# A decoder step on one core: the first block's conditioning made in two halves, with half granules of the input projection behind each

## The chip, the core and the metric

One core of a Trainium2 chip runs the whole step as one program. The metric is the device time of one execution in microseconds (us), from the first to the last instruction and what lies around them. All data is fp32. A product of two fp32 matrices is made of three matmuls on rounded parts (hi x wh, lo x wh, hi x wl), each with 128 x 128 weights and 288 moving columns.

## The reference, cut to what matters

```python
sc = jax.nn.silu(c)                                   # c: 9 sequences x 2048
mod = jnp.einsum('bd,sde->sbe', sc, w_ada[l]) + b_ada[l][:, None, :]
sh0, scl0, gt0 = jnp.split(mod[0], 3, axis=-1)        # shift, scale, gate, 2048 each
h = modulate(rmsnorm(x, norm_pre[l, 0]), sh0, scl0)   # h = xn * (1 + scale) + shift
proj = h @ w_in                                       # 288 rows, 2048 -> 6160
```

There are 256 prompt rows and 32 sample rows. This document is about the first microseconds: the modulation of layer 0's first sub-layer (w_ada), the modulated activations h, and their product with w_in. Everything later (attention, state-space layer, two MLPs) is unchanged.

## The kernel before

Activations lie with features on partitions: x is eight tiles ("pairs") of 128 x 2 x 288, so 256 features each. Four blocks of 512 features (two pairs) are numbered kb = 0 to 3. Weights come from memory in granules of 512 x 512 (1 MB, a tile raw of 128 x 4 x 512, 8 KB in a row per partition). split_w casts half a granule on ScalarE (wh) and subtracts on VectorE or, for the second half, on GpSimd (wl). gran_mm makes half a granule's output columns (pr = 0 or 1, a PSUM pair of two banks): 24 matmuls for a whole granule's four feature chunks; a granule is 48.

**Conditioning.** The shift and the scale of one block of 512 features are two times four granules of w_ada, 8 MB. ada_mm makes a step of one granule: four fp32 matmuls that lie side by side in four 32-column strips of the array and sum in one PSUM bank over the eight steps. ada_end then copies the bank to SBUF (ScalarE), turns it by four transposes (TensorE), reduces (VectorE) and ada_out makes the tiles mod A and mod B. For block 0 this is the generator first = ada_group(...), driven from the loop "for n in range(8)" that also loads x and sums its squares (Stat); r is the reciprocal norm. It loads through rawp, three buffers of a whole granule. For all later blocks it is the stream cond = ada_stream(groups, ...), whose tiles alternate between rawp and one buffer raw2; each next(cond) makes one step and sets off the load two steps ahead. ended tells which groups are complete.

**Projections.** The list slots sets the order: first eight granules (u = 0 to 7) of block 0, then eight of block 1, each closed alone (start = stop = 1): block 0 copies the PSUM pair to an SBUF accumulator proj (A.copy), block 1 adds to it (V.tensor_add). Later slots sum longer in PSUM. In front of slot 0, make_block(0) builds h of the two pairs, its rounded parts hi and lo (split_a); low_rank(kb) is a small product at the first slot of each block. The orders of TensorE and of SyncE, which issues all loads, are written out by hand (manual_schedule); those of ScalarE, VectorE and GpSimd are a planner's. fill_in puts 0.42 steps of cond at each of four points of a slot (i < 15). At the end of slots 6, 14 and 15 the stream is driven until the next block's group has ended, and make_block builds that block. The load of slot i+2 is issued and slot i+1 is split at the start of slot i. SyncE stands still at a load whose buffer is not free, with all later loads behind it.

Of the kernel before, what the change touches and what calls it, by code (L numbers as in the profile page):

```python
# [9 lines left out]
F32 = mybir.dt.float32  # L10
# [3 lines left out]
OP = mybir.AluOpType  # L14
AX = mybir.AxisListType
# [5 lines left out]
NT = NP + NB * TS  # L21
# [8 lines left out]
V_ADA = 0  # L30
V_PRE = 192
V_POST = 256
# [129 lines left out]
def build(tc, nc, d):  # L162
    mm = nc.tensor.matmul
# [67 lines left out]
    def split_a(t):  # L231
        hi = c2("hi", F32R)
        A.copy(hi, t)  # L233
        lo = c2("lo", F32R)
        V.tensor_sub(lo, t, hi.bitcast(F32))  # L235
        return hi, lo
# [15 lines left out]
    def chunks(pairs):  # L252
        return [(hi[:, c, :], lo[:, c, :]) for hi, lo in pairs for c in range(2)]
# [10 lines left out]
    def ada_src(blocks, n):  # L264
        l, s, nb = blocks[n // 4]
        return d["g_ada"][l, s, nb, n % 4]
# [12 lines left out]
            ada_out(blk, red[:, :, 9 * slot:9 * slot + 9])  # L279
        yield  # L280

    def ada_out(blk, v):
        l, s, nb = blk
        k0 = V_ADA + (l * 2 + s) * 48 + 4 * nb
        b = vec[:, k0:k0 + 4][:, :, None].to_broadcast([128, 4, 9])
        eb = nb % 4
        g0 = (l * 2 + s) * 16 + 4 * eb
        sl = slice(4 * eb, 4 * eb + 4)
        if nb < 4:
            V.tensor_add(mod("B", l, s)[:, sl, :], v, b)  # L290
            return
        t = ep.tile([128, 4, 9], F32, name=nm("adat"), tag="adat", bufs=2)
        V.tensor_add(t, v, b)
        if nb < 8:
            w = vec[:, V_PRE + g0:V_PRE + g0 + 4][:, :, None].to_broadcast([128, 4, 9])
            V.scalar_tensor_tensor(mod("A", l, s)[:, sl, :], t, 1.0, w, op0=OP.add, op1=OP.mult)
        else:
            w = vec[:, V_POST + g0:V_POST + g0 + 4][:, :, None].to_broadcast([128, 4, 9])
            V.tensor_mul(mod("G", l, s)[:, sl, :], t, w)

    def ada_group(blocks):
        ps = bank()
        for n in range(4 * len(blocks)):
            raw = load(ada_src(blocks, n))
            ada_mm(ps, blocks, n, raw)
            if n < 4 * len(blocks) - 1:
                yield
        for _ in ada_end(ps, blocks):
            pass
        yield 0  # L310
# [46 lines left out]
    ended = set()  # L357

    def drain(gen, n=10 ** 9):
        for _ in range(n):  # L360
            if next(gen, "end") == "end":
                break
# [83 lines left out]
    def make_h(p, r, l, s, act=False):  # L446
        t = h_norm(p, r)
        h_mod(t, p, l, s, act)
        return t
# [252 lines left out]
    x = []  # L702
# [5 lines left out]
        return t  # L708

    st = Stat(7)  # L710
    first = ada_group([(0, 0, 0), (0, 0, 4)])
    for n in range(8):
        if n < 4:
            x += [x_load(d["xT"], p) for p in (2 * n, 2 * n + 1)]
        if 2 <= n < 6:
            for p in (2 * n - 4, 2 * n - 3):
                st.add(x[p])
        if n == 6:
            r = st.rstd(keep=True)
        drain(first, 1)  # L720
    drain(first)


    def kgran_(hv, acts, acc, u, first, done=None):
# [456 lines left out]
    def w_load(i):  # L1181
        if i < len(slots):
            k, u, kb = slots[i][:3]
            raws[i] = load(d[k][u, kb])

    def w_split(i):
        if i < len(slots):
            hvs[i] = split_w(raws.pop(i), 2, (None, G))

    hops = {}  # L1190
    hts = {}

    def make_block(kb):
        hops[kb] = []
        for pp in range(2):
            t = make_h(2 * kb + pp, r, 0, 0, act=True)
            x[2 * kb + pp] = None
            hops[kb].append(split_a(t))
            hts[2 * kb + pp] = t

    def low_rank(kb):
        gp = bank((128, NT))
# [24 lines left out]
    def step(g, n=1):  # L1227
        for _ in range(n):
            next(g, None)
# [20 lines left out]
    att = attention()  # L1250
    m = Mlp(0)
    with tc.manual_schedule(engines={mybir.EngineType.PE, mybir.EngineType.SP}):
        w_load(0)
        w_load(1)
        step(cond, 3)
        make_block(0)
        w_split(0)
        for i, (k, u, kb, start, stop, init, fin) in enumerate(slots):
            inp = k == "g_in"
            w_load(i + 2)  # L1260
            if i == OUT + 6:
                sub.weights()
            m.before(len(slots) - 1 - i)
            if 0 <= i - OUT - 8 < 4:
                x[2 * (i - OUT - 8):2 * (i - OUT - 8) + 2] = [x_load(d["xT"], 2 * (i - OUT - 8) + k) for k in range(2)]
            if i == 14:
                sm = cst(C_SMASK)
                causal = cst(C_CAUSAL, 384)
            if inp and u == 0:
                low_rank(kb)  # L1270
            w_split(i + 1)
            if i + 1 in (OUT, OUT + 8):
                for nkb in ((0, 1) if i + 1 == OUT else (2, 3)):
                    while 2 * nkb + 1 not in mixed or nkb // 2 not in ready:
                        step(att)
                    oacts[nkb] = chunks([split_a(mixed.pop(2 * nkb + n)) for n in range(2)])
            hv = hvs.pop(i)
            acts = chunks(hops[kb]) if inp else oacts[kb]
            acc = proj if inp else yacc
            for pr in range(2):  # L1280
                pi = 2 * u + pr
                if start:
                    ps[pr] = pair()
                gran_mm(ps[pr], hv, pr, acts, start, stop, 0)
                fill_in(i)
                gran_mm(ps[pr], hv, pr, acts, start, stop, 1)
                if stop:
                    o_ = ps[pr][:, :, :NT]
                    if init:
                        acc[pi] = c2("acc")  # L1290
                        A.copy(acc[pi], o_)
                    else:
                        V.tensor_add(acc[pi], acc[pi], o_)  # L1293
                    if fin and inp:
                        projected(pi, acc[pi])
                    elif fin:
                        late.append(pi)
                fill_in(i)
            if i in (6, 14, 15):
                n = {6: 1, 14: 2, 15: 3}[i]  # L1300
                while n - 1 not in ended:
                    next(cond)
                make_block(n)
            while len(late) > 2:
                pi = late.pop(0)
                sub.add(pi, yacc[pi])
        while late:
            pi = late.pop(0)
            sub.add(pi, yacc[pi])
        drain(cond)  # L1310
# [639 lines left out]
```

## Time and profile before

| | |
|---|---|
| median of 3 runs | 2856.94 us (2851.47 to 2861.42) |
| the profiled execution, its own time | 2850.12 us |
| its span, first to last instruction | 2848.4 us |
| granted TensorE clock, mean | 0.978 |
| TensorE busy | 2725.4 us, 96% of the span |
| moved by DMA | 662.99 MB |

Times in the rows are microseconds from the start of the span. PE is TensorE, DVE VectorE, ACT ScalarE, POOL GpSimd, SP SyncE; an operation is named by its line, its output tile and its input tiles. A clock of 1.0 is full speed, 0.5 half speed. A DMA share of 1.0 says that all 16 DMA engines are busy.

### The profile page before, as it was taken

The numbers are of one execution on the slowest core, as the hardware profiler recorded it, in microseconds if no ns is written. First come the engines' busy times: TensorE is split into PE (matmuls) and PEld (weight loads), VectorE is DVE, ScalarE is ACT, GpSimd is POOL, SyncE is SP. The second block draws the span as 40 slices with busy tenths as digits, with TensorE's granted clock in tenths as the row PEclk, the third lists the DMA queues.
The fourth block names the chain that finished last, engine by engine and source line by source line (L and its number), as shares of the span: only waits on it lengthen the run. The fifth ranks groups of instructions, "written<-read, shape, count | busy, mean of one in ns | idle before, by whom it ended". The sixth has DMA issues, their size and how long they took to land.

```text
span 2848.4 us, 53282 instructions
## 1 busy us (share of the span) xinstructions
PE 2725.4 (96%) x22334; PEld 2458.7 (86%) x22334; DVE 1740.8 (61%) x2656; ACT 1079.6 (38%) x1389; POOL 381.8 (13%) x478
## 2 busy tenths in 40 slices
PE   6999998999999999999999799997999999999997
PEld 3788786777999999999999578874899999999997
DVE  2356556547866657687775767757545555555556
ACT  3344433334433333333433343333433333333332
POOL 1233242340010000000011322102000000000003
PEclk8999999999999999999999799998999999999998
DMA  9887686675677767765555698866564444444442
GB/s 351 341 320 296 261 283 240 240 291 196 251 253 245 260 237 281 274 240 196 189 192 198 223 323 304 311 240 250 197 236 165 168 169 165 163 163 165 169 170 93
DMA packets 167233, 662.99 MB, mean 233 GB/s; under 512 B 21440, under 2 KB 41280, under 8 KB 108368
## 3 DMA queue, kind: packets, MB, share of 16 engines
q1 hardware_dynamic: 158000, 633.56, 61.8%
q0 software_dynamic: 7840, 23.67, 2.1%
q8 instruction: 175, 2.87, 0.4%
q10 hardware_dynamic: 1152, 2.36, 0.2%
q14 instruction: 66, 0.54, 0.1%
HBM read 622.74 MB, written 36.77 MB: 232 GB/s over the span
## 4 chain that ended last, share of the span: by engine, by line
PE 85%; DVE 6%; DMA 5%; issue 2%; ACT 1%; POOL 1%; SPq 0%; POOLq 0%; DVEq 0%; ACTq 0%
PE mm L248 25%; PE mm L250 24%; PE mm L249 24%; PE b L260 5%; DMA raw<-g_ada 1%; PE b L1683 1%; DMA adaw<-g_ada 1%; DVE wl L227 1%; DMA raw<-g_glu 1%; PE b L1753 1%; PE b L1471 1%; DMA x<-xT 1%; PE b L1758 0%; PE b L494 0%; ACT wh L225 0%
## 5 line engine op out<-in xcount | busy, mean ns | idle before, releaser
L248 PE MATMUL mm<-hi,wh 128*128 128x288 f32 x5632 | 1693.7, 301 | 26.2 <-DVE acc L735 11.9
L249 PE MATMUL mm<-lo,wh 128*128 128x288 f32 x5632 | 1669.2, 296 | 4.5 <-DVE lo L611 4.4
L250 PE MATMUL mm<-hi,wl 128*128 128x288 f32 x5632 | 1668.1, 296 | 2.3 <-DVE wl L227 1.8
L248 PEld LDWEIGHTS mm<-hi,wh 128*128 128x128 f32 x5632 | 1062.9, 189 | 166.0 <-issue 98.6
L225 ACT CAST wh<-raw 128x1024 fp32r<-128x1024 f32 x692 | 719.3, 1049 | 1066.5 <-PE mm L249 859.6
L227 DVE TENSOR_TENSOR wl<-raw,wh 128x1024 fp32r<-128x1024 f32 x628 | 765.5, 1231 | 548.4 <-ACT wh L225 539.4
L249 PEld LDWEIGHTS mm<-lo,wh 128*128 128x128 f32 x5632 | 1064.6, 189 | 6.3 <-DVE lo L611 5.7
L250 PEld LDWEIGHTS mm<-hi,wl 128*128 128x128 f32 x5632 | 1063.5, 189 | 3.7 <-DVE wl L227 3.0
L735 DVE TENSOR_TENSOR acc<-acc,mm 128x576 f32<-128x576 f32 x304 | 227.8, 751 | 148.4 <-PE mm L250 147.5
L227 POOL TENSOR_TENSOR wl<-raw,wh 128x1024 fp32r<-128x1024 f32 x64 | 163.7, 2559 | 364.0 <-ACT wh L225 343.8
L260 PE MATMUL b<-raw,cpad 128*32 128x512 f32 x1104 | 156.1, 639 | 27.9 <-DMA raw<-g_ada 27.7
L482 POOL TENSOR_TENSOR acc<-acc,modG 128x512 f32<-128x512 f32 x32 | 39.4, 1231 | 979.1 <-ACT sq L391 836.9
L660 DVE TENSOR_TENSOR relu<-relu 128x576 f32<-128x576 f32 x64 | 48.3, 755 | 67.4 <-ACT relu L659 67.4
L260 PEld LDWEIGHTS b<-raw,cpad 128*32 128x32 f32 x1104 | 22.3, 110 | 60.0 <-issue 30.2
L1293 DVE TENSOR_TENSOR acc<-acc,mm 128x576 f32<-128x576 f32 x40 | 30.0, 751 | 70.0 <-PE mm L250 70.0
L659 ACT ACTIVATE relu<-mm 128x576 f32<-128x576 f32 x64 | 41.5, 649 | 79.7 <-PE mm L250 79.5
L233 ACT CAST hi<-relu 128x576 fp32r<-128x576 f32 x64 | 43.2, 675 | 72.4 <-DVE relu L660 72.4
L260 PE MATMUL b<-adaw,cpad 128*32 128x512 f32 x432 | 66.2, 651 | 0.8 <-DMA adaw<-g_ada 0.8
L235 DVE TENSOR_TENSOR lo<-relu,hi 128x576 fp32r<-128x576 f32 x64 | 48.3, 755 | 29.4 <-ACT hi L233 28.7
L1499 POOL DMA_DIRECT2D s5k<-lag x16 | 12.1, 756 | 284.8 <-ACT lag L1498 158.9
L1560 POOL DMA_DIRECT2D s5c<-lc x32 | 17.4, 543 | 225.8 <-DVE lc L1559 219.9
L1683 PEld LDWEIGHTS b<-h,rb 128*128 128x128 f32 x256 | 35.9, 220 | 12.4 <-ACT h L1673 7.9
(356 smaller groups left out, 1588.1 us busy)
## 6 DMA issues: line engine op xcount, KB each, us to landing
raw<-g_ada SPq DMA_DIRECT2D x138, 1024.0 KB, 5.2
raw<-g_up SPq DMA_DIRECT2D x128, 1024.0 KB, 4.8
raw<-g_dn SPq DMA_DIRECT2D x128, 1024.0 KB, 4.9
adaw<-g_ada SPq DMA_DIRECT2D x216, 256.0 KB, 6.3
raw<-g_in SPq DMA_DIRECT2D x48, 1024.0 KB, 6.8
raw<-g_glu SPq DMA_DIRECT2D x64, 512.0 KB, 6.6
raw<-g_out SPq DMA_DIRECT2D x16, 1024.0 KB, 6.7
s5b<-ft SPq DMA_DIRECT2D x128, 64.0 KB, 4.1
```

Source lines behind the costliest of these rows:

```text
L225: A.copy(wh, r)
L227: (lo[hf] or V).tensor_sub(wl, r, wh.bitcast(F32))
L233: A.copy(hi, t)
L235: V.tensor_sub(lo, t, hi.bitcast(F32))
L248: mm(o, wh[:, k4 % n, cs], hi, start=first and k4 == 0, stop=False)
L249: mm(o, wh[:, k4 % n, cs], lo, start=False, stop=False)
L250: mm(o, wl[:, k4 % n, cs], hi, start=False, stop=last and k4 == nk - 1)
L260: mm(ps[32 * k4:32 * k4 + 32, :], cpad[:, 4 * kg + k4, 18 - 9 * slot:50 - 9 * slot], raw[k4] if isinstance(raw, list) else raw[:, k4, :], ...
L659: A.activation(t, ps[pr][:, :, :NT], AF.Relu)
L660: V.tensor_mul(t, t, t)
L735: V.tensor_add(acc[pi], acc[pi], ps[:, :, :NT])
L1683: mm(vps[ch][ri][:, q, :], rb[q // 2][:, q % 2, ri, :], h4[p][:, q, c, :], start=True, stop=True)
```

## The change

first and second are now generators of ada_half: the same eight steps, each for 256 of the 512 output features. A step's tile comes as two loads of 128 x 2 x 256 (256 KB each, 1 KB in a row) into general SBUF tiles, up to three steps ahead, not into rawp. The sum over the steps takes 256 columns of a PSUM bank; two transposes follow, and ada_out writes half a block's mod A and B. After the first half, only pair 0 is built; eight half granules (the 256 features of pair 0, 12 matmuls for each pr, loads of 512 KB) run with one half step of second behind each (two behind the first), then pair 1 is built, low_rank(0) follows, and eight half granules of pair 1 add to proj. In these the steps of cond run, three for every two half granules, and cond starts only there. Slots 0 to 7 of the list fall away; slot 8 goes on as before.

```diff
+    def ada_half(blocks, hf, depth=3):
+        ps = bank()
+        held = []
+        def ahead(n):
+            if n < 4 * len(blocks):
+                ts = [c2("adaw", shape=(128, 2, 256)) for _ in range(2)]
+                for k, t in enumerate(ts):
+                    nc.sync.dma_start(t, ada_src(blocks, n)[:, 2 * k:2 * k + 2, 256 * hf:256 * hf + 256])
+                held.append(ts)
+        for n in range(depth):
+            ahead(n)
+        yield
+        for n in range(4 * len(blocks)):
+            ts = held.pop(0)
+            slot, kg = divmod(n, 4)
+            for k4 in range(4):
+                mm(ps[32 * k4:32 * k4 + 32, :256], cpad[:, 4 * kg + k4, 18 - 9 * slot:50 - 9 * slot], ts[k4 // 2][:, k4 % 2],
+                   start=n == 0, stop=n == 4 * len(blocks) - 1, tile_position=(0, 32 * k4))
+            ahead(n + depth)
+            yield
+        ev = c2("adae", shape=(128, 256))
+        A.copy(ev, ps[:, :256])
+        yield
...
-    first = ada_group([(0, 0, 0), (0, 0, 4)])
-    for n in range(8):
+    first, second = (ada_half([(0, 0, 0), (0, 0, 4)], hf) for hf in range(2))
+    for n in range(10):
...
-        w_load(0)
-        w_load(1)
-        step(cond, 3)
-        make_block(0)
-        w_split(0)
...
+        half_load(0)
+        half_load(1)
+        drain(second, 1)
+        drain(first)
+        hops[0] = []
+        make_pair(0, 0)
+        half_split(0)
+        for j in range(16):
+            part, u = divmod(j, 8)
+            half_load(j + 2)
+            if j == 7:
+                drain(second)
+                make_pair(0, 1)
+                drain(cond, 1)
+            if j == 8:
+                low_rank(0)
+            half_split(j + 1)
+            hv = hhv.pop(j)
+            for pr in range(2):
+                pi = 2 * u + pr
+                o_ = pair()
+                gran_mm(o_, hv, pr, chunks([hops[0][part]]), True, True)
+                o_ = o_[:, :, :NT]
+                if part:
+                    V.tensor_add(proj[pi], proj[pi], o_)
+                else:
+                    proj[pi] = c2("acc")
+                    A.copy(proj[pi], o_)
+                if pr and not part:
+                    drain(second, 2 if j == 0 else 1)
+                elif part and (pr or j % 2):
+                    step(cond)
+            if j == 14:
+                while 0 not in ended:
+                    next(cond)
+                make_block(1)
         for i, (k, u, kb, start, stop, init, fin) in enumerate(slots):
+            if i < 8:
+                continue
...
-            if i in (6, 14, 15):
-                n = {6: 1, 14: 2, 15: 3}[i]
+            if i in (14, 15):
+                n = {14: 2, 15: 3}[i]
```

half_load(j) loads half granule j into the first half of a rawp buffer (from j = 16 on: w_load(j - 8), a whole granule); half_split(j) splits it, with the subtraction on GpSimd for odd j. The slots 8 and on are reached with the stream's budget at zero.

## Rows read from the trace of the kernel before

**Rows 1.** Table by stage: start:end, length, busy times (instructions), clock, DMA share, GB/s.

```profile
0.00:28.00 28.00, 12.06 (x56) 2.96 (x56) 6.86 (x12) 11.35 (x18) 0.97 (x5) 1.00 0.92 356
28.00:45.50 17.50, 9.10 (x44) 1.99 (x44) 8.41 (x15) 6.79 (x9) 3.75 (x2) 0.52 0.95 377
45.50:80.00 34.50, 33.78 (x249) 26.48 (x246) 5.89 (x5) 10.17 (x13) 8.55 (x4) 1.00 0.90 334
80.00:114.80 34.80, 34.80 (x257) 27.63 (x255) 14.50 (x18) 15.54 (x21) 10.01 (x4) 1.00 0.90 339
```

**Rows 2.** Chain of work that ended last, first 50 us: start, duration, what.

```profile
24.66 7.42 DMA raw<-g_ada
32.13 1.98 PE b L260 x8
34.13 0.59 ACT adae L270
34.77 1.13 PE b L274 x4
35.92 0.70 DVE adar L277
...
37.21 0.60 ACT h L440
...
38.65 0.68 ACT hi L233
...
39.35 2.62 DVE lo L235
```

**Rows 3.** TensorE's timeline: start, duration, operation, times, idle time before it.

```profile
40.80 1.94 PE L260 MATMUL b<-raw,cpad 128*32 128x512 f32 x8 [4.92 <-DMA raw<-g_ada]
...
44.93 0.66 PE L1207 MATMUL b<-h,wglr 128*32 128x288 f32 x8
45.52 0.40 PE L248 MATMUL mm<-hi,wh 128*128 128x288 f32 x1
...
57.93 0.30 PE L249 MATMUL mm<-lo,wh 128*128 128x288 f32 x1
58.06 0.29 PE L250 MATMUL mm<-hi,wl 128*128 128x288 f32 x1
...
62.45 0.29 PE L250 MATMUL mm<-hi,wl 128*128 128x288 f32 x1
62.67 1.06 PE L260 MATMUL b<-raw,cpad 128*32 128x512 f32 x8
...
63.91 0.30 PE L249 MATMUL mm<-lo,wh 128*128 128x288 f32 x1
...
114.82 0.69 PE L1207 MATMUL b<-h,wglr 128*32 128x288 f32 x8
```

**Rows 4.** VectorE's timeline, the first modulated pair: start, duration, operation.

```profile
25.66 0.76 DVE L432 TENSOR_TENSOR h<-x,r 128x576 f32<-128x576 f32 x1
```

**Rows 5.** DMA view of 11 to 20 us, where all 16 engines are busy.

```profile
DMA packets 941, 3.80 MB, mean 422 GB/s; under 512 B 109, under 2 KB 109, under 8 KB 621
```

**Rows 6.** DMA view of 1546.5 to 1551.5 us: loads with rows of 2 KB.

```profile
DMA packets 1115, 2.02 MB, mean 405 GB/s; under 512 B 127, under 2 KB 127, under 8 KB 1115
```

**Rows 7.** The tile raw from 36 to 115 us: count, duration ns min/median/max, first and last start.

```profile
L260 PE MATMUL b<-raw,cpad x128: 592/617/1063, 40.8 to 112.5; 128*32 128x512 f32 x128
...
L225 ACT CAST wh<-raw x17: 1028/1048/1059, 37.7 to 110.0; 128x1024 fp32r<-128x1024 f32 x17
L337 SPq DMA_DIRECT2D raw<-g_ada x16: 327/328/657, 41.4 to 113.2; - x16
...
L227 POOL TENSOR_TENSOR wl<-raw,wh x9: 2380/2476/2564, 38.8 to 111.1; 128x1024 fp32r<-128x1024 f32 x9
...
DMA to landing us min/median/max: 4.8/7.5/11.3
```

**Rows 8.** Groups of instructions by line, 45.5 to 114.8 us: busy us, mean ns, idle before.

```profile
L1291 ACT COPY acc<-mm 128x576 f32<-128x576 f32 x15 | 9.6, 638 | 31.1 <-PE mm L250 31.1
```

More of the change, by code (lines that the diff above doesn't have):

```diff
@@ L280, in ada_end, with ada_out @@
         yield
-    def ada_out(blk, v):
+    def ada_half(blocks, hf, depth=3):
[21 more added lines that the diff above has]
+        yield
+        pt = bank()
+        for c in range(2):
+            nc.tensor.transpose(pt[:, 128 * c:128 * c + 128], ev[:, 128 * c:128 * c + 128], idn)
+        red = ep.tile([128, 4, 32], F32, name=nm("adar"), tag="adar", bufs=1)
+        V.tensor_reduce(red[:, :2], pt[:, :256].rearrange("p (c j m) -> p c m j", c=2, j=4), axis=AX.X, op=OP.add)
+        for slot, blk in enumerate(blocks):
+            ada_out(blk, red[:, :2, 9 * slot:9 * slot + 9], 2 * hf, 2)
+        yield
+    def ada_out(blk, v, o=0, n=4):
         l, s, nb = blk
-        k0 = V_ADA + (l * 2 + s) * 48 + 4 * nb
-        b = vec[:, k0:k0 + 4][:, :, None].to_broadcast([128, 4, 9])
+        k0 = V_ADA + (l * 2 + s) * 48 + 4 * nb + o
+        b = vec[:, k0:k0 + n][:, :, None].to_broadcast([128, n, 9])
         eb = nb % 4
         g0 = (l * 2 + s) * 16 + 4 * eb
-        sl = slice(4 * eb, 4 * eb + 4)
+        sl = slice(4 * eb + o, 4 * eb + o + n)
         if nb < 4:
@@ L291, in ada_out @@
             return
-        t = ep.tile([128, 4, 9], F32, name=nm("adat"), tag="adat", bufs=2)
+        t = ep.tile([128, 4, 9], F32, name=nm("adat"), tag="adat", bufs=2)[:, :n]
         V.tensor_add(t, v, b)
         if nb < 8:
-            w = vec[:, V_PRE + g0:V_PRE + g0 + 4][:, :, None].to_broadcast([128, 4, 9])
+            w = vec[:, V_PRE + g0 + o:V_PRE + g0 + o + n][:, :, None].to_broadcast([128, n, 9])
             V.scalar_tensor_tensor(mod("A", l, s)[:, sl, :], t, 1.0, w, op0=OP.add, op1=OP.mult)
         else:
-            w = vec[:, V_POST + g0:V_POST + g0 + 4][:, :, None].to_broadcast([128, 4, 9])
+            w = vec[:, V_POST + g0 + o:V_POST + g0 + o + n][:, :, None].to_broadcast([128, n, 9])
             V.tensor_mul(mod("G", l, s)[:, sl, :], t, w)
@@ L720, in build @@
         drain(first, 1)
-    drain(first)
     def kgran_(hv, acts, acc, u, first, done=None):
@@ L1191, in build, with make_pair @@
     hts = {}
+    def make_pair(kb, pp):
+        t = make_h(2 * kb + pp, r, 0, 0, act=True)
+        x[2 * kb + pp] = None
+        hops[kb].append(split_a(t))
+        hts[2 * kb + pp] = t
     def make_block(kb):
@@ L1195, in make_block @@
         for pp in range(2):
[L1196 to L1199, printed above, removed]
+            make_pair(kb, pp)
     def low_rank(kb):
@@ L1252, in build, with half_load, half_split @@
     with tc.manual_schedule(engines={mybir.EngineType.PE, mybir.EngineType.SP}):
-        w_load(0)
-        w_load(1)
-        step(cond, 3)
-        make_block(0)
-        w_split(0)
+        hraw, hhv = {}, {}
+        def half_load(j):
+            if j < 16:
+                part, u = divmod(j, 8)
+                hraw[j] = rawp.tile([128, 4, 512], F32, name=nm("raw"), tag="raw")
+                nc.sync.dma_start(hraw[j][:, :2], d["g_in"][u, 0][:, 2 * part:2 * part + 2])
+            else:
+                w_load(j - 8)
+        def half_split(j):
+            if j < 16:
+                hhv[j] = split_w(hraw.pop(j), 1, (G if j % 2 else None,))
+            else:
+                w_split(j - 8)
+        half_load(0)
[6 more added lines that the diff above has]
+        for j in range(16):
+            part, u = divmod(j, 8)
+            half_load(j + 2)
[14 more added lines that the diff above has]
+                    V.tensor_add(proj[pi], proj[pi], o_)
+                else:
+                    proj[pi] = c2("acc")
[8 more added lines that the diff above has]
+                make_block(1)
         for i, (k, u, kb, start, stop, init, fin) in enumerate(slots):
+            if i < 8:
+                continue
             inp = k == "g_in"
```

## The prediction

> **What bounds the kernel now.** I read the table by stage first [rows 1]. TensorE is busy 12.06 of the first 28 us and 9.10 of the next 17.5; from 45.5 it is busy 33.78 of 34.5 us and then all of 34.8. So the program has a short head in which TensorE waits, and then a fixed pile of TensorE work. A change of the head is worth what it moves the start of that pile, less the work that it pushes behind the start, less any new wait in the pile. The reader should also see the DMA share: 0.90 to 0.95 in every row. The second resource is nearly full, also where TensorE is the bound.
>
> The chain of waits [rows 2] says what the head is made of: the eighth tile of w_ada, issued at 24.66, lands at 32.08; its step ends at 34.1; then copy, transposes, reduce, h, hi, and lo at 39.35 with 2.62 us. TensorE's timeline [rows 3] completes it: two steps of cond from 40.80, the low-rank product at 44.93, the first projection matmul at 45.52, and slot 8 at 114.82. By then cond has made 128 / 8 = 16 steps [rows 7].
>
> **Prices from the timeline.** Projection matmuls start every 0.13 us (57.93, 58.06), so a half granule of 24 costs 3.2 us. A step takes from 62.45 to 63.91 less two matmuls, 1.46 - 0.26 = 1.2 us: 1.0 of its own and 0.2 of changing over [rows 3]. A half step streams 256 columns where the trace shows 512; the nearest row is the low-rank product, also eight records of 32-column tiles, with 288 columns: 44.93 to 45.52, 0.6 us [rows 3]. Half step: 0.6 + 0.2 = 0.8 us.
>
> **A. The first half's data.** Four of the eight megabytes leave the head: 4.19 MB at 422 GB/s [rows 5] are 9.9 us. The four that stay come in rows of 1 KB, which the trace shows at no size worth reading. A row of 2 KB takes 16 engines x 5 us / 988 packets (1115 less 127 tiny ones) = 81 ns [rows 6]; one of 8 KB takes 16 x 8192 / 422 = 311 ns [rows 5]. The straight line through both has 4 ns fixed, so 1 KB is 43 ns, 381 GB/s, and 4.19 MB take 11.0 us: 1.1 more. Bounds: nothing fixed, 0; all of the 81 ns fixed, 202 GB/s and 10.8 more. I take 1.1, since 2 KB is the nearest row and shows no loss worth the name. Landing: 32.1 - 9.9 + 1.1 = 23.3 (before: 32.1). At half clock a step took 1.94 us [rows 3], so half a step 1.0: end at 24.3 instead of 34.1. The issues are 16 where there were 8, at 0.33 us each [rows 7]; SyncE no longer stands at a rawp buffer there, and 16 x 0.33 = 5.3 us hide under 11 us of data.
>
> That split speaks against a rule of the Trainium skill (Perfetto Trace Analysis, DMA Optimizations): transfers get efficient with size, and "Small DMAs (< 2KB) have significant per-transfer overhead". The skill's page on bandwidth (DMA: Bandwidth & Descriptors, Anatomy of one DMA) gives an estimate of 2.0 us plus bytes over 436 GB/s for each load; were the sixteen loads served one after another, the half would take 42 us. The trace disagrees for queued loads of 256 KB, at 405 GB/s [rows 6].
>
> **B. From the last step to the first projection.** Before: 34.13 to 41.97 for pair 0 (7.8 us), then pair 1, two steps and low-rank until 45.52. After: pair 0 alone, with half the copy (-0.3), two transposes (-0.6) and half the reduce (-0.3): at most 6.6 us. With nothing in between (ScalarE's gap before 38.65; lo at 0.76, the h row of the same shape [rows 4], instead of 2.62) it is 4.4 [rows 2]. So the projections start at 28.7 to 30.9; I take 29.5, 16.0 before the old 45.5. x and r do not get in the way: pair 0 was normed at 25.66 [rows 4], and as many bytes stand ahead of the last x loads as before (six halves for three tiles).
>
> **C. What now lies behind the start.** Eight half steps of second, 6.4 us. The copy that TensorE waits for (half of 0.59, and 0.1 to hand over) and two transposes (half of 1.13) [rows 2], 1.0. Low-rank, 0.7. The two steps of cond that were in front, 2.4. And the clock: the stage from 28 to 45.5 has 0.52, so full clock for (0.52 - 0.50) / 0.50 = 0.04 of 17.5 us, 0.7 us at its end: it rose at 44.8, 4.0 us after TensorE resumed at 40.80 [rows 1, 3]. After the change TensorE stands still from 24.3 to 29.5, nothing warms it as the two steps did, and 4.0 us at half speed lose 2.0 (bounds 0, if the clock is still up, and 2.0). Sum 12.5. The head is worth 16.0 - 12.5 = 3.5 us if nothing else waits.
>
> **D. Pair 1.** At j = 7 its reduce, mod, h, hi, lo (4 to 6 us by B) run under one half granule and low-rank (3.9 us), behind which j = 8 is queued on TensorE; and ScalarE has casts and copies of proj in its queue. 0 to 2 us of wait; I take 1.
>
> **E. The second eight half granules.** They are 8 x 3.2 us; with them run 12 steps, and 3 more are forced at j = 14, since the group of block 1 counts as ended only in the 13th. 25.6 + 15 x 1.2 = 43.6 us of TensorE. What must land meanwhile: 13 granules of w_ada (two are there), 5 half granules, and slot 8's granule, which stands in the queue ahead of the last steps: 16.5 x 1.049 = 17.3 MB, 400 GB/s and more where the old stages used 334 to 339 [rows 1]. The first of these loads needs the buffer of half granule 9, which GpSimd frees: cast 1.0 and subtraction 2.48, 3.5 us in; then 4.8 - 2.5 = 2.3 us to get going [rows 7]. At 422 GB/s (41.0 us) the last tile lands at 46.8; at 338 / 0.90 = 376 (46.0 us) at 51.8; it is wanted at 42.4. So 4.4 to 9.4 us of wait, or 0.9 if the planner splits half granule 9 earlier. I take 6, near the full rate, as the queue seldom runs dry there. Most of it falls on the forced steps. SyncE adds to it: it stands at raw2 until a step has run, with the next granules behind it.
>
> **F. At nothing.** Sixteen additions to proj (0.76 us each, by the row of that shape [rows 4]) replace no copy but come on top: VectorE is busy 5.89 of 34.5 us there [rows 1]. A PSUM pair must be emptied within 1.6 + 0.8 us instead of 3.2; the copy takes 0.64 [rows 8] and a cast ahead of it 1.05 [rows 7], so it fits; without that room each of the 32 would cost a few tenths. The number of casts and subtractions stays. After slot 8 the stream is one step behind (15 against 16), 1.2 us that are paid later.
>
> **Sum.** 3.5 - 1 - 6 = 3.5 us lost, so 2853.6 for an execution like the profiled one (2850.12, of which 2848.4 are the span). The median of the runs stands 6.8 above that execution: 2856.9 + 3.5 = 2860.4. A measurement of this kernel can tell about 0.3%, 8.6 us, from no change; this is inside.
>
> **Rivals.**
> 1. Forecast: the head is shorter and the second part's loads take it back. 2855 to 2866. Chance 0.55.
> 2. The loads keep up: C alone, 3.5 us gained, and up to 8.5 if B takes 4.4 us, the clock stays up and the wait of D is gone: 2848 to 2854. For it: with this stream TensorE lost only 34.5 - 33.78 = 0.7 us in 69 before [rows 1]. Against: E asks for 17.3 MB in 42.4 us, 408 GB/s from its first moment, and the old stages moved 339 with the DMA engines busy for 0.90 of the time [rows 1]. Chance 0.22, of which 0.07 passes 0.3%.
> 3. Slower, by the 1 KB rows: if they have a fixed cost, the first half lands up to 9.7 us later than I took: 2870. It decides from 262 GB/s down (5 us later). Against: 2 KB rows run at 405. Chance 0.10.
> 4. Slower, by E alone: at 9.4 us, with one wait long enough that the clock falls, as it had from 28 us on [rows 1], 2.0 more: 2866. Against: the longest single wait should be about 4 us. Chance 0.08.
> 5. The change does not bring pair 0 forward as meant, because x, r and the norm end last and not the modulation: start at 31.5, 2862 to 2863. Against: 25.66 [rows 4]. Chance 0.05.
>
> **Numbers.** Forecast 2860.4, its own range 2855 to 2866; the range that takes in the fast end of 2 and most of 3 is 2849 to 2870. Faster by over 0.3%: 0.07 (rival 2). Slower: 0.08 of rival 3, 0.04 of 4, 0.03 of 1: 0.15. Same: 0.78.
>
> **What would show it.** A: the last 256 KB tile lands near 23. B: first projection matmul near 29.5, at half clock. C: eight half steps of 0.6 us. D: a gap of a microsecond ahead of the ninth half granule. E: waits on raw from w_ada of some 6 us, most of them after the fifteenth half granule; slot 8's low-rank product at 115 to 118. Wrong would be: slot 8 before 110 (loads keep up), or a landing after 28 (rows of 1 KB).

## The result: slower by 0.73%, and the profile after

| | before | after |
|---|---|---|
| median, same chip | 2852.65 us (6 runs, 2851.27 to 2861.42) | 2874.50 us (6 runs, 2872.71 to 2877.31) |
| ratio, 95% interval | | 1.0073 [1.0060, 1.0086] |
| span of the profiled execution | 2848.4 us | 2875.4 us |
| granted TensorE clock, mean | 0.978 | 0.974 |

The forecast was 2860.4 us, 2849 to 2870: 3.5 us lost, counted from a median of 2856.94 for the kernel before. Measured side by side, 21.9 us are lost. In later measurements the kernel before had medians of 2852.5 to 2853.7, so its profiled execution (2850.12) lies about 3 us low; that of the kernel after (2877.31) is the slowest of its six, 2.8 above their median. So of the 27 us between the two spans, some 5 belong to these two executions, and the profiles don't show where.

The table by stage of the kernel after, with the columns of [rows 1]:

```profile
core 0: us, PE busy (x) PEld busy (x) DVE busy (x) ACT busy (x) POOL busy (x), PEclk, DMA share, GB/s
0.00:25.00 25.00, 12.60 (x56) 4.54 (x56) 4.73 (x8) 10.29 (x16) 0.97 (x5) 0.86 0.93 328
25.00:34.00 9.00, 1.91 (x21) 0.78 (x19) 7.05 (x13) 4.64 (x8) 2.85 (x1) 0.87 1.08 391
34.00:68.00 34.00, 31.82 (x243) 26.99 (x244) 8.41 (x8) 16.67 (x23) 9.46 (x4) 0.93 0.49 171
68.00:95.00 27.00, 26.23 (x193) 19.27 (x192) 11.90 (x20) 6.55 (x8) 3.38 (x3) 1.00 0.88 337
95.00:112.00 17.00, 12.74 (x92) 7.68 (x92) 8.12 (x16) 3.86 (x5) 3.87 (x2) 1.00 0.99 390
112.00:135.00 23.00, 17.32 (x116) 9.72 (x116) 7.09 (x11) 5.87 (x8) 5.00 (x2) 0.85 0.85 349
```

TensorE is idle 7 us in the second row, and 10 us in the last two, where before it was idle 0 us from 80 to 114.8 [rows 1]. Between them, from 34 to 68 us, it is busy for 31.82 of 34 us, but the DMA share is 0.49, where the kernel before had 0.90 from 45.5 to 80 us [rows 1]. The DMA engines had been the second full resource; here they lose half a stage. After 88 us TensorE waits for tiles of w_ada; that the two belong together is shown below, by e15 against e13.

TensorE's timeline after, to be read beside [rows 3]: the head, and the largest waits before slot 8.

```profile
21.49 3.83 PE L421 MATMUL b<-sq,ones 128*128 128x288 f32 x8
25.24 1.07 PE L301 MATMUL b<-adaw,cpad 128*32 128x256 f32 x16
...
33.84 0.61 PE L248 MATMUL mm<-hi,wh 128*128 128x288 f32 x1 [6.60 <-ACT hi L233]
...
115.46 1.93 PE L260 MATMUL b<-raw,cpad 128*32 128x512 f32 x8 [5.56 <-DMA raw<-g_ada]
...
125.97 0.67 PE L1245 MATMUL b<-h,wglr 128*32 128x288 f32 x8
```

Waits of TensorE from 34 to 130 us after, by what it waited for: us in all, times, longest.

```profile
PE b L260 <- DMA raw<-g_ada: 10.7, 8, 5.6
...
PE mm L250 <- POOL wl L227: 1.5, 1, 1.5
PE b L310 <- ACT adae L306: 0.5, 1, 0.5
```

The loss comes in two places. Slot 8's low-rank product is at 125.97 instead of 114.82 [rows 3], with 15 steps of the stream made instead of 16: 11.2 + 1.2 = 12.4 us. From there to 752 us the distance between the two kernels' projection matmuls grows from 11.1 to 24.1 us, 1.2 of it the step that is owed. (Another 3 us come between 1600 and 2000 us; they differ between the kernels measured here and were not followed.)

VectorE and GpSimd before the first projection, after:

```profile
26.93 0.46 DVE L406 SCALAR_TENSOR_TENSOR r<-t,r 128x288 f32<-128x288 f32 x1
...
28.16 1.22 DVE L227 TENSOR_TENSOR wl<-raw,wh 128x1024 fp32r<-128x1024 f32 x1
29.29 2.90 DVE L468 TENSOR_TENSOR h<-x,r 128x576 f32<-128x576 f32 x1
...
28.72 2.85 POOL L227 TENSOR_TENSOR wl<-raw,wh 128x1024 fp32r<-128x1024 f32 x1 [27.21 <-ACT wh L225]
```

h <- x,r takes 2.90 us, where the same operation took 0.76 [rows 4]. It ends 0.62 us after GpSimd's subtraction does (32.19 and 31.57). And r itself is only ready at 27.39.

Why nothing moves from 43 to 50 us is seen in three more answers. SyncE's issues after, in order of time:

```profile
36.46 0.90 SPq L291 DMA_DIRECT2D adaw<-g_ada  x2
50.49 0.34 SPq L1298 DMA_DIRECT2D raw<-g_in  x1
```

SyncE's waits from 36 to 51 us after, with the columns of the waits above:

```profile
SPq L1298 <- POOL wl L227: 13.1, 1, 13.1
```

The DMA view of 37 to 50 us after, busy tenths in 40 slices:

```profile
DMA  9999989899986421000000000000000000000000
```

SyncE waits 13.1 us at the load of a half granule (L1298) for a buffer, until GpSimd has subtracted from it; the last loads land, and from 43 us on nothing moves. This stall is not the whole of the 0.49: in e2 and e15 below no load waits longer than 5.6 us in that stage, and the share is still 0.58 and 0.66. Until the stream of later blocks starts (its first loads go out at 64.14 us), the program asks for little.

### The profile page after: what moved, and what is told of

Read it like the earlier page. It is cut to its first block, busy times and chain, and to the rows that moved or that the text cites. A ratio compares the mean times of both kernels' runs of the same rounds, so it can differ in the third digit from the quotient of the medians.

```text
span 2875.4 us, 53484 instructions
## 1 busy us (share of the span) xinstructions
PE 2738.6 (95%) x22398; PEld 2470.2 (86%) x22398; DVE 1756.2 (61%) x2676; ACT 1082.8 (38%) x1392; POOL 379.3 (13%) x478
## 4 chain that ended last, share of the span: by engine, by line
PE 84%; DVE 6%; DMA 5%; ACT 2%; issue 2%; POOL 1%; SPq 0%; POOLq 0%; ACTq 0%; DVEq 0%
PE mm L248 25%; PE mm L249 24%; PE mm L250 24%; PE b L260 5%; DMA raw<-g_ada 1%; DMA adaw<-g_ada 1%; DMA raw<-g_glu 1%; PE b L1771 1%; DVE wl L227 1%; DMA raw<-g_in 1%; ACT wh L225 1%; PE b L1559 1%; PE b L1841 1%; PE b L530 0%; PE b L1846 0%
## 5 line engine op out<-in xcount | busy, mean ns | idle before, releaser
L260 PE MATMUL b<-raw,cpad 128*32 128x512 f32 x1040 | 140.9, 614 | 14.6 <-DMA raw<-g_ada 14.6
L235 DVE TENSOR_TENSOR lo<-relu,hi 128x576 fp32r<-128x576 f32 x64 | 48.4, 756 | 29.5 <-ACT hi L233 29.4
L1771 PEld LDWEIGHTS b<-h,rb 128*128 128x128 f32 x256 | 35.5, 218 | 10.8 <-ACT h L1761 7.8
```

Source lines behind the costliest of these rows:

```text
L260: mm(ps[32 * k4:32 * k4 + 32, :], cpad[:, 4 * kg + k4, 18 - 9 * slot:50 - 9 * slot], raw[k4] if isinstance(raw, list) else raw[:, k4, :], ...
L1771: mm(vps[ch][ri][:, q, :], rb[q // 2][:, q % 2, ri, :], h4[p][:, q, c, :], start=True, stop=True)
```

## Experiments

Each was timed beside the kernel before on the same chip. "Offset at slot 8" is how much later than in the profile of before the 129th matmul of the kind hi x wl starts, the first in slot 8's granule; after it is 11.1. It is read from one execution each. How far these scatter is seen in e8, whose instructions up to there are those of the kernel before but for one step: its first projection starts at 47.32 us, before's at 45.52.

### One part of the change alone

**e4_halves.** The conditioning in two halves, both ahead of make_block(0); projections by whole granules from slot 0 on, as before. The cut is against the kernel before; ada_half is that of the change.

```diff
-    drain(first)
+    drain(second, 10)
...
+        drain(first)
+        drain(second)
         step(cond, 3)
         make_block(0)
```

> The conditioning alone in two halves of 256 features, with its 256 KB loads and rows of 1 KB, both halves ahead of block 0; the projections as in the kernel before, in whole granules. Theory, harmless rows: 8.4 MB at 43 ns a row take 2 us more than before, first projection matmul at 46 to 49, total within 4 us of before. Rival, costly halves: first projection after 53, total 8 us or more above before.

2858.87 us, 1.0017 [1.0008, 1.0027]; offset at slot 8 only 0.6. From slot 8 to 760 us ScalarE, VectorE and GpSimd execute the same operations in the same order as before, and TensorE still loses about 4 us more. Where these come from is open: both profiled executions are low ones (e4's by 4.7 us against its median), so the low profile of before doesn't account for them. The first projection is at 47.13, as expected; in all the halves cost some 6 us between medians, which lies between the two expectations. They are not what costs 22 us.

**e11_half_granules, e14_deep_half.** Conditioning as before, but sixteen half granules with sums in SBUF, each in a buffer of its own, two half granules loaded ahead, a step of the stream behind 14 of them (e11). In e14, two half granules share a buffer, and loads run two such pairs ahead, as whole granules do before:

```diff
+            if j % 2 == 0:
+                for n in (j + 4, j + 5):
+                    half_load(n)
-            half_load(j + 2)
...
-                hraw[j] = rawp.tile([128, 4, 512], F32, name=nm("raw"), tag="raw")
+                if j % 2 == 0:
+                    hbuf[0] = rawp.tile([128, 4, 512], F32, name=nm("raw"), tag="raw")
+                hraw[j] = hbuf[0][:, 2 * (j % 2):2 * (j % 2) + 2]
```

> The half granules alone: conditioning of the whole first block ahead of the projections, by whole granules as in the kernel before; then both pairs and the sixteen half granules with sums in SBUF, each in a buffer of its own as in the change, the sixteen steps of the stream and the budget as before. Theory that a half granule in a whole buffer turns the buffers over twice as often as they can be loaded and split: 6 to 12 us of waits for weight parts before slot 8, 2862 to 2868. Rival, half granules cost nothing by themselves and the loss is that of the compressed stream: slot 8 within 2 us of the kernel before, 2853 to 2857.

> Half granules alone, with the conditioning of whole granules ahead, and loads two pairs ahead in shared buffers. Look-ahead theory: the 8.9 us of waits for weight parts go to under 2, slot 8 from 124.6 to 116 to 118, 2855 to 2859. Rival (half granules are late in the queues of ScalarE and VectorE, whatever the loads do): slot 8 at 122 or later, 2864 to 2868.

e11: 2867.52 us, 1.0053 [1.0038, 1.0069], offset 11.8. e14: 2854.67 us, 1.0004 [0.9995, 1.0014], offset 4.0. TensorE's waits from 45 to 130 us, e11 and then e14:

```profile
PE mm L250 <- POOL wl L227: 4.7, 4, 1.9
PE mm L248 <- ACT wh L225: 2.4, 2, 1.3
PE mm L250 <- DVE wl L227: 1.8, 3, 0.7
```

```profile
PE b L260 <- DMA raw<-g_ada: 1.9, 3, 0.9
PE b L1246 <- DVE h L480: 1.6, 1, 1.6
```

Of e11's 8.9 us of waits for weight parts nothing is left in e14. A half granule with its step lasts 3.2 + 1.2 = 4.4 us on TensorE, so two of them ahead are 8.8 us; in e11 a load into raw, whole or half, took 4.7 to 9.3 us from issue to landing (median 5.7), and cast and subtraction follow (1.05, then 1.22 or 2.4). Issues of half granules in e11 (L1299) stand behind the stream's (L373), which SyncE can only make when a step has freed its buffer:

```profile
80.65 0.33 SPq L373 DMA_DIRECT2D raw<-g_ada  x1
82.09 0.33 SPq L1299 DMA_DIRECT2D raw<-g_in  x1
86.36 0.33 SPq L373 DMA_DIRECT2D raw<-g_ada  x1
86.78 0.38 SPq L1299 DMA_DIRECT2D raw<-g_in  x1
```

So the half granules by themselves cost 14 us with the change's look-ahead, and 1.4 (not told from 0) with the old one. The pairing alone isn't it (e5 and e7 against e10, below).

### One repair at a time in the changed kernel

**e1_phase and e9_budget** give the stream back its old places from slot 8 on: e1 makes the sixteenth step ahead of slot 8, e9 lets it come a quarter of a slot later.

```diff
+        step(cond)
+        budget["ada"] = -0.56
```

and in e9 only

```diff
+        budget["ada"] = 0.44
```

> The changed kernel with one more step of cond ahead of slot 8 and the stream's budget set to -0.56, so that the stream stands at slot 8 as in the kernel before (16 steps) and every later instruction of TensorE comes in the old order. Theory, shifted interleave: the loss after slot 8 (13 us between 127 and 670 us in the profiles) is the other order of stream steps and attention, so it goes, and only the 11 to 13 us up to slot 8 stay: about 2865 against 2852 for before. Rival, backlog of loads: the loads stay behind after slot 8 whatever the order, so the time stays near that of the changed kernel, 2872 to 2877.

> The changed kernel with one line more: the stream's budget stands at 0.44 instead of zero when slot 8 begins, so that the sixteenth step comes a quarter of a slot into slot 8 and all later steps fall where they do in the kernel before. Order theory: what is lost between 127 and 700 us falls from 13 us of the profile to about the 5 of the kernels that have the old order; the sixteenth step may wait 1 to 3 us for its tile; 2874.5 - 6 to 8, so 2866 to 2869. Rival, as with the extra step ahead of slot 8: the wait for the tile takes it back, 2872 to 2875.

e1: 2873.19 us, 1.0062 [1.0047, 1.0077], offset 19.8. e9: 2871.55 us, 1.0066 [1.0052, 1.0080], offset 10.4. In e1 the distance grows by only 5.1 us from slot 8 to 752 us (13.0 after), but slot 8 comes 8.7 us later, 1.2 of them the step itself and the rest waits for w_ada (one alone of 6.66 us). In e9 the distance grows by 8.1. Both gain less than I expected, 2 and 4 us by the distance of their medians from the kernel before's, and the intervals overlap with the one of the kernel after. e1 lies where its second expectation has it, e9 between its two. In this kernel the step's tile is late, and giving it its old place brings the wait forward.

**e2_act.** ScalarE's order in the sixteen half granules by hand, with the first cast ahead of the copy of the sums.

```diff
-    with tc.manual_schedule(engines={mybir.EngineType.PE, mybir.EngineType.SP}):
+    with tc.manual_schedule(engines={mybir.EngineType.PE, mybir.EngineType.SP, mybir.EngineType.Activation}):
...
+        half_split(0)
         drain(first)
         hops[0] = []
         make_pair(0, 0)
-        half_split(0)
```

> The changed kernel with ScalarE's order in the half granules written by hand (the cast of the next half granule ahead of the copies of this one, half granule 0 cast before pair 0 is built); nothing else moves. Theory, ScalarE's order: the cast of half granule 3, whose data lands at 35.7, runs only at 47.0, so its buffer keeps SyncE standing from 37 to 50 us with the DMA engines half idle; with the cast early the loads go on, the stream's first tiles come about 6 us earlier, and slot 8 starts at 117 to 121 instead of 126. Rival, concentration: 15 steps of the stream within eight half granules ask for more than the DMA engines move, wherever they start; slot 8 stays at 124 to 127.

2870.64 us, 1.0059 [1.0042, 1.0076], offset 7.1. That is 4 us less than after by medians, with intervals that overlap; slot 8 comes at about 122, between the two expectations. GpSimd's first subtraction comes only at 31.85, h <- x,r takes 0.75 us, and the first projection starts 3 us earlier than after (0.8 of this because the last half step ends at 25.48 in this execution, 26.31 after). The timelines of VectorE and TensorE in e2:

```profile
28.47 0.75 DVE L468 TENSOR_TENSOR h<-x,r 128x576 f32<-128x576 f32 x1
...
30.88 0.61 PE L248 MATMUL mm<-hi,wh 128*128 128x288 f32 x1 [4.46 <-ACT hi L233]
```

**e3_spread.** The stream starts at j = 0 and makes one step behind each half granule from j = 1 on (15 in all).

```diff
+            if j == 0:
+                drain(cond, 1)
...
-                elif part and (pr or j % 2):
-                    step(cond)
+                if pr and j:
+                    step(cond)
```

> The changed kernel with the steps of cond spread over all sixteen half granules (one behind each from the second on, its first two loads issued at j = 0) instead of three for every two of the last eight. Theory, concentration: the waits on raw from w_ada between 70 and 126 us (10.7 us in the changed kernel) fall under 3 us and slot 8 starts at 114 to 119. Rival, ScalarE's order: the buffers that its late casts hold are now wanted by the stream too, so the waits only move into the first eight half granules and slot 8 stays at 124 or later.

2874.13 us, 1.0067 [1.0052, 1.0082], offset 13.3: no gain at all. But the wait has changed its name. TensorE's groups from 34 to 135 us in e3:

```profile
L250 PE MATMUL mm<-hi,wl 128*128 128x288 f32 x136 | 43.6, 320 | 12.0 <-POOL wl L227 6.0 <-DVE wl L227 6.0
...
L260 PE MATMUL b<-raw,cpad 128*32 128x512 f32 x128 | 17.8, 628 | 0.0
```

No wait for w_ada is left; 12.0 us of waits for weight parts stand in its place. This is the short look-ahead, which the packed stream had covered: in e16 below, where ScalarE's order is the planner's too but the look-ahead is mended, no such wait is among those listed from 34 to 130 us.

**e5_pair and e6_pair_act.** Two half granules share a buffer, still loaded two half granules ahead; e6 has ScalarE's order as well.

> The changed kernel, but two half granules in a row share one buffer of a whole granule, a half each, so that one of the three buffers stays free for the stream. Buffer theory (a half granule holds a buffer as long as a whole one, SyncE stands at it from 36.94 to 50.49 with the loads of second and cond behind it, and this is what TensorE waits for after 88 us): DMA share of 34 to 68 us from 0.49 to 0.8 or more, waits on w_ada before slot 8 from 10.7 us to under 4, slot 8's low-rank product from 126.0 to about 119, and 2874.5 - 7 = 2867 or less. Rival, the planner's order of ScalarE alone (half granule 3 cast late): the buffers are no matter, slot 8 stays at 124 to 126, 2871 to 2875.

> The paired buffers and ScalarE's order by hand in the sixteen half granules (the first cast ahead of the copy of the sums, the others where the code has them). If the two causes add: first projection at 31 as with the order alone, slot 8 at 113 to 117, and 4 us less than with the paired buffers alone, 2860 to 2864. If they are one cause (late casts hold buffers), the same as the better of the two alone, 2867 to 2871.

e5: 2874.53 us, 1.0073 [1.0058, 1.0089], offset 13.0. e6: 2870.78 us, 1.0059 [1.0044, 1.0074], offset 7.0. The buffer theory falls: the freed buffer gains nothing over the kernel after, nor over e2. In e5 SyncE still waits 13.0 us at a half granule, and the share from 34 to 68 us is 0.59, not 0.8.

### The order of the stream, in the kernel before

**e8_phase15.** No half granules, no halves: the sixteenth step is left out ahead of slot 8 and the budget set to zero there.

```diff
+            if len(calls) == 33:
+                budget["ada"] = 0.0
+            if 30 < len(calls) < 33:
+                return
```

(calls counts the points of fill_in for the stream; the 33rd is the first of slot 8.)

> The kernel before, with one thing changed: the sixteenth step of the stream is not made ahead of slot 8, and the budget stands at zero there, as in the changed kernel. No data is later than before. Order theory (the stream's steps fall at other places among the attention's work and so make TensorE wait there): slot 8 starts 1.2 us earlier, and 8 to 13 us are lost between 127 and 700 us, 2860 to 2865. Rival (the loss after slot 8 comes from late loads or is spread over the attention at random): within 3 us of the kernel before, 2850 to 2856.

2862.72 us, 1.0032 [1.0021, 1.0044]; offset 0.0 at slot 8. So 9.4 us are lost by this alone. The largest wait shows one way; TensorE in e8 and in after:

```profile
388.39 0.63 PE L1034 MATMUL b<-st,qm 128*32 128x256 f32 x6
...
394.65 1.91 PE L1034 MATMUL b<-st,qm 128*32 128x256 f32 x10 [5.62 <-DMA st<-s_gla]
```

```profile
399.02 0.63 PE L1069 MATMUL b<-st,qm 128*32 128x256 f32 x6
...
404.38 1.92 PE L1069 MATMUL b<-st,qm 128*32 128x256 f32 x10 [4.72 <-DMA st<-s_gla]
```

SyncE's issues ahead of it, in after and in before:

```profile
393.94 0.33 SPq L373 DMA_DIRECT2D raw<-g_ada  x1
...
396.54 1.53 SPq L1032 DMA_DIRECT2D st<-s_gla  x3
```

```profile
389.05 0.91 SPq L997 DMA_DIRECT2D st<-s_gla  x2
395.76 0.33 SPq L337 DMA_DIRECT2D raw<-g_ada  x1
```

With the old order that state's load goes out ahead of the stream's load, 6.6 us before TensorE starts on it at 395.61; with the new one it stands behind the stream's load on SyncE, which in after waits 10.8 us for a step to free its buffer, and TensorE waits. Part of this comes back: the wait ahead of the transposes of ons, 4.55 us in before (433.2), is 1.52 in e8 (443.6). The other waits between 115 and 770 us differ from before's in the same places in e8 and in after (new: 1.95 us at the low-rank product, 1.33 ahead of the first heads); in all TensorE is idle 41.6 us there in e8 and 33.8 in before. That sum alone doesn't tell the orders apart: e13 below, which has the old order, is idle 40.4 us there. In the profiles the distance grows by 12.2 us from slot 8 to 752 us in e8, and by 13.0 in after. Over all kernels here it grows by 8.9 (e5) to 14.4 us (e3) with the new order and by 1.3 (e14) to 10.0 us (e11) with the old one, so the order is not all that decides it.

### Repairs together

**e10_act_spread, e7_all, e15_deep_act, e16_deep_planned, e13_deep_all** combine the edits above. All have the old budget (in e15, as in e9, the sixteenth step comes a quarter of a slot into slot 8). e10: ScalarE by hand, sixteen spread steps. e7: also paired buffers. e13: e7 with loads two pairs ahead. e15: e13 with the stream packed as in the change. e16: e13 with ScalarE left to the planner.

> Paired buffers, ScalarE's order by hand, and a step of the stream behind each of the sixteen half granules, 16 in all, with the budget of the stream as in the kernel before when slot 8 begins. From slot 8 on TensorE's order is that of the kernel before. If what is lost after slot 8 comes from the other order, it is gone here: an offset of 0 to 4 us at slot 8 stays that or grows by 4 to 5 as in the kernel with whole granules, 2853 to 2861. If the later loss comes from a backlog of loads that these kernels share, the offset at the end is 8 us or more above that at slot 8: 2863 or more.

> As the run with everything together (paired buffers, ScalarE's order by hand, sixteen spread steps, old budget), but without the pairing: each half granule holds a whole buffer again. If the buffers matter once the stream's loads are spread: TensorE waits for weight parts wl 9 to 12 us ahead of slot 8 instead of 5.7, 2867 to 2870. If only ScalarE's late casts made the buffers scarce: as with everything together, 2861 to 2865.

> As the run with everything together, but half granules are loaded two pairs ahead (1 MB ahead of the pair in use, as the kernel before does with whole granules), not two half granules ahead. Look-ahead theory (load issued 5 to 8 us before landing, then cast 1.05 and subtraction 1.2 to 2.4, against a period of 4.4 us for a half granule with its step, so that two half granules ahead is too short): the waits for weight parts before slot 8 fall from 6.8 us to under 2, slot 8 comes 4 to 6 us earlier, 2857 to 2860. Rival (GpSimd's 2.4 us and ScalarE's queue are late by themselves): the waits stay above 5, 2862 to 2865.

> The change with the loads two pairs ahead, ScalarE's order by hand and the budget of 0.44 at slot 8, but with the stream's steps in the second eight half granules only, as in the change. If the compressed stream by itself asks for more than the queue brings (the prediction's step E): waits on w_ada of 5 us or more stay before slot 8, 2864 to 2869. If it was the short look-ahead that held the stream up: waits on w_ada under 3 us, 2857 to 2862.

> Loads two pairs ahead, sixteen spread steps, the old budget, but ScalarE's order left to the planner. If ScalarE's order is worth only the head (GpSimd subtracts beside VectorE's h, 2.90 us instead of 0.75, so that the first projection starts at 33.5 instead of 31.5): slot 8 some 3 us later than with the order by hand, 2853 to 2856. If the planner's late casts also hold up the pairs' loads: waits for weight parts come back, 5 us or more before slot 8, 2857 to 2862.

| kernel | stream | ahead | ScalarE | offset at slot 8 | ratio, 95% interval |
|---|---|---|---|---|---|
| after | packed | 2 halves | planner | 11.1 | 1.0073 [1.0060, 1.0086] |
| e15 | packed | 2 pairs | by hand | 10.8 | 1.0065 [1.0050, 1.0080] |
| e10 | spread | 2 halves | by hand | 6.4 | 1.0037 [1.0023, 1.0051] |
| e7 | spread | 2 halves, paired | by hand | 3.9 | 1.0033 [1.0022, 1.0045] |
| e16 | spread | 2 pairs | planner | -0.1 | 1.0011 [1.0001, 1.0021] |
| e13 | spread | 2 pairs | by hand | -4.5 | 0.9993 [0.9983, 1.0003] |

e7, e15 and e16 each take one thing away from e13: the look-ahead is worth 0.40% (11 us), the spread stream 0.72% (20 us; e15 also has its sixteenth step later), ScalarE's order 0.18% (5 us; here the two intervals just overlap). What the old budget is worth in e13 was not tried. They don't add, since each cause stands behind another: with two halves ahead and the planner's order the spread gains nothing (e3), and with a packed stream the kernel stays at 1.0065 though look-ahead, ScalarE's order and budget are all mended (e15), no better than ScalarE's order alone (e2). e7 itself came out, if only just, as its second expectation had it: 2863.13 us, and its distance from before, 3.9 at slot 8, is 11.9 at the end. So the old order does not by itself end the loss after slot 8. TensorE's waits in e15 and in e13, from 32 to 130 us:

```profile
PE b L260 <- DMA raw<-g_ada: 7.9, 5, 2.7
PE b L1245 <- DVE h L480: 3.7, 2, 2.4
```

```profile
PE mm L248 <- ACT hi L233: 4.4, 1, 4.4
PE b L260 <- DMA raw<-g_ada: 1.5, 2, 0.9
```

And the stage from 34 to 68 us, first e15, then e13:

```profile
34.00:68.00 34.00, 33.00 (x261) 27.79 (x261) 8.34 (x14) 18.98 (x27) 7.17 (x3) 0.96 0.66 235
```

```profile
34.00:68.00 34.00, 33.12 (x278) 25.22 (x281) 4.35 (x4) 14.50 (x20) 8.06 (x4) 0.98 0.99 381
```

In e13 the DMA engines are full, 381 GB/s, and TensorE waits 1.5 us; in e15 they have little to load in that stage, 235 GB/s, and later TensorE waits 7.9 for the stream.

e16 shows what ScalarE's order does. The planner puts four casts ahead of h; GpSimd subtracts for 6.14 us, VectorE stands twice, and the first projection is at 36.40. VectorE and GpSimd in e16:

```profile
27.43 1.22 DVE L227 TENSOR_TENSOR wl<-raw,wh 128x1024 fp32r<-128x1024 f32 x1
29.15 2.79 DVE L227 TENSOR_TENSOR wl<-raw,wh 128x1024 fp32r<-128x1024 f32 x1 [0.50 <-ACT wh L225]
31.86 2.89 DVE L468 TENSOR_TENSOR h<-x,r 128x576 f32<-128x576 f32 x1
...
27.99 6.14 POOL L227 TENSOR_TENSOR wl<-raw,wh 128x1024 fp32r<-128x1024 f32 x2 [26.48 <-ACT wh L225]
```

**e12_before_ve.** The kernel before, with the first granule's second subtraction on VectorE.

```diff
-            hvs[i] = split_w(raws.pop(i), 2, (None, G))
+            hvs[i] = split_w(raws.pop(i), 2, (None, G if i else None))
```

> The kernel before, with the subtraction of the first granule's second half on VectorE instead of GpSimd, so that GpSimd stands still while lo of pair 0 is made. If GpSimd at work is what stretches a VectorE subtraction from 0.76 to 2.62 us: lo takes 0.8 and the first projection starts 0.6 to 1.9 us earlier (VectorE has 1.22 more to do), 2851 to 2853, not to be told from no change. If not: lo stays at 2.6 and the start is up to 1.2 us later, 2853 to 2855.

2852.82 us, 0.9996 [0.9987, 1.0005], not told from no change. VectorE ahead of the first projection in e12, and GpSimd:

```profile
39.81 0.75 DVE L235 TENSOR_TENSOR lo<-h,hi 128x576 fp32r<-128x576 f32 x1
41.15 3.38 DVE L227 TENSOR_TENSOR wl<-raw,wh 128x1024 fp32r<-128x1024 f32 x1
...
40.90 2.55 POOL L227 TENSOR_TENSOR wl<-raw,wh 128x1024 fp32r<-128x1024 f32 x1 [39.39 <-ACT wh L225]
```

lo takes 0.75 us, 2.62 in [rows 2]. But GpSimd's next subtraction now meets VectorE's next one, which takes 3.38 where 1.22 is usual. The stall has moved. The first projection starts at 46.50, 1 us later than in before's profile; with 47.32 in e8, whose head is unchanged, that is within the scatter.

## Why the prediction was wrong, step by step

**A, the first half's data: right.** The DMA engines moved 392 GB/s from 11 to 20 us with rows of 1 KB (381 worked out), and the last tile, issued at 17.7, landed 5.5 us later, near 23 (23.3 worked out). So rival 3, the rows, is out. (The section of the Trainium skill that the prediction names for 2.0 us plus bytes gives this fit for loads that GpSimd issues; here SyncE issues them.) The last half steps ran at 25.24 to 26.31 instead of ending at 24.3, not for data: eight matmuls of the sums of squares stood in front of them on TensorE (21.49, 3.83 us at half clock).

**B, from the last step to the projections: right kind, wrong size.** 29.5 predicted, at most 30.9; 33.84 measured, 4.3 us late. 2.0 of these are the late last step, and r ended only at 27.39, behind the late sums of squares, where pair 0 was normed at 25.66 before [rows 4]: "x and r do not get in the way" failed. From the last step to the first projection 5.2 us were predicted, with 6.6 as the upper bound, and 7.5 measured: VectorE made a weight subtraction of 1.22 us ahead of h, and h cost 2.90 instead of 0.76, with GpSimd at work beside VectorE. With ScalarE's order by hand, where GpSimd isn't, these are 5.4 us (e2, from 25.48 to 30.88), and the projections start at 30.88 (e2) to 31.53 (e13), near the 31.5 of rival 5. ScalarE's order is worth some 4 us (e2) to 5 us (e16 against e13) in all.

**C and D: right.** A half step's record took 0.64 us, 0.6 predicted. The clock was 0.50 from 33.8 to 38.2 us, a loss of 2.2, 2.0 predicted. Pair 1 cost 0.5 us of wait, 1 predicted.

**E, the second eight half granules: right kind, wrong size.** 43.6 us of work and 6 of waits were forecast; 55.1 us were measured (70.87 to 125.97), with 9.3 of waits. The other 2.2 are clock: after the longest wait, 5.56 us, the clock was 0.50 from 115.4 to 120 us, and a step took 1.93 us instead of 1.06. That is what rival 4 described (9.4 us, one long wait, 2.0 for the clock); what spoke against it, a longest wait of about 4 us, did not hold. The step that failed is the choice of 6 out of 4.4 to 9.4, "near the full rate, as the queue seldom runs dry there". At the start of this part the stream was no later than assumed: three of its loads were out by 68.13, two were assumed. But the queue moved 340 GB/s on average, at a DMA share of 0.87, and from 115.4 to 119 the share was 0.19: from 68 to 126 us SyncE waited over 20 us for steps of TensorE to free buffers, the term that the prediction named last and gave no number. That packing the stream makes this wait is shown by e15 against e13, where it costs 20 us.

**F, at nothing: failed.** "The number of casts and subtractions stays" is true, but half_load(j + 2) is half as far ahead in time as w_load(i + 2). In the kernel after itself this shows little, 1.5 us of waits for weight parts, since the packed stream stands in front. It is worth 11 us once nothing hides it (e7 to e13) and 12 us with the half granules alone (e11 to e14).

**After slot 8: failed.** The forecast carried one step of 1.2 us over and held the rest unchanged. But the stream's budget at slot 8 decides between which pieces of the attention its steps and loads fall; a shift of 0.44 of a step costs 9.4 us in a kernel that has nothing else changed (e8). e8's profile loses 12.2 us there, after's 13.0 (both against the low profile of before), with waits in the same places. That the old order alone gives back only 2 to 4 us in the changed kernel (e1, e9), and that kernels with the old order still lose up to 10 us after slot 8 (e11), suggests that the late loads would have cost part of it anyway; that was not tried apart, and how the 13.0 us divide in the changed kernel is open.

**The sum.** In the profiles 4.3 us beyond the forecast came in B, 5.5 in E and some 12 after slot 8; between medians the forecast is off by 18 in all. C's 3.5 us of gain "if nothing else waits" is close to what e13 shows, 4.5 at slot 8; since offsets of single executions scatter by 2 us, and e13's head starts 2 us later than C had it, the closeness is in part luck. By the end of the program e13's median is 2.6 us below before's, not told from no change. So rival 2 describes, at most, the kernel that the change could have been.

## What to carry to other kernels

When work is cut into halves, a look-ahead counted in pieces is cut in half with it: check it in microseconds against issue, landing and conversion, before buffers or engines are suspected. Where a second resource is nearly full, no stage may leave it idle: what a stage doesn't load comes back as a wait much later, under another name, and mending one cause alone may gain nothing because the next stands right behind it. And a background stream that is interleaved by a running budget has a phase: an edit long before can move all later steps, so bring the phase back, or measure it by itself in the old kernel, before the rest is judged.

## What the hardware showed

A VectorE operation on two SBUF tiles that came up while GpSimd subtracted stood until GpSimd had ended: h <- x,r ended 0.62 us after it in after and in e16 (32.19 and 31.57; 34.75 and 34.13), for an operation that takes 0.75 us alone. An addition with one of its inputs in PSUM did not stand: acc <- acc,mm took 0.75 us at 94.64 in after, inside a subtraction of GpSimd's from 94.11 to 96.48. The Trainium skill (GPSIMD Engine Reference, Specifications) says that GpSimd shares its SBUF interface with VectorE and that instructions with two SBUF inputs contend; these rows agree.
